# Two of the three matmuls of a split product made one of 512 columns, with the main sum and the corrections apart in a bank

## The chip, the cores and the metric

The kernel runs on one NeuronCore of a Trainium2 chip. The metric is the device time of one execution in microseconds (us). Engines: PE is TensorE, which multiplies, PEld its weight loads; DVE is VectorE, ACT ScalarE, POOL GpSimd, SP the engine that starts the DMAs. A bank is one of eight pieces of PSUM, TensorE's output memory: 2 KB on each of 128 partitions, 512 fp32 numbers.

## The reference, cut to what matters

256 tokens x of 1024 numbers go through two hybrid layers and then through one block of another kind, all in fp32:

```python
def hybrid_layer(x, norm_g, w_in, ...):
    p = split_columns(rmsnorm(x, norm_g) @ w_in)
    qk = silu(causal_dwconv(concat([p['ml_q'], p['ml_k']]), ...))
    hm = mlstm_chunkwise(...)
    hg = gla_chunked(heads(p['gla_q']), heads(p['gla_k']), ...)
    dk = rmsnorm(heads(p['dsa_k']), dsa_k_g)
    hd = dsa_sparse_attention(dq, dk, ..., topk)
    y = concat([y_ml, y_gla, y_dsa]) @ w_out
    return x + y

h = h + 0.5 * swiglu(rmsnorm_2(h), w_gate, w_up, w_down)
z = rmsnorm_2(h) @ w_in
# attention and a spatial gating of z, each through its w_branch, gated by sigmoid(n @ w_gate + b_gate), through w_out
h = h + 0.5 * swiglu(...)
```

Nearly all of the work is products of the 256 normed tokens with weight matrices that come from HBM once.

## The kernel before, in words

**Products.** A product keeps fp32's accuracy by splitting both factors into a rounded half and what is left of it (`hi` and `lo` of the weights, `xh` and `xl` of x), both in TensorE's faster fp32 type, and adding up three matmuls: wh with xh, wh with xl, wl with xh (`mm3`, L136).

**Units.** Weights come in units of 512 KB, in the order of their use, 362 in all (`weights`, L101): SP starts the DMA, ACT rounds the unit to `hi` (L112), DVE subtracts to get `lo` (L113). Five `hi`/`lo` pairs and three raw units fit, so casts run a few units ahead of PE.

**Two kinds of projection.** `proj_a` (L143) holds x in the array and moves 512 weight columns; its output is [token, 512 columns], in one bank for each of the two tokens' halves (t = 0 and 1; the prediction calls them the first and second token). `proj_b` (L173) holds 128 x 128 weights in the array and moves the 256 tokens; its output is [128 columns, n, 256 tokens], n = 2 column groups of one unit each in one bank. A unit of `proj_b` has eight k-steps of 128 rows each, 24 matmuls.

**PSUM.** Accumulators of the projections come from a pool `pj` of four banks (`acc`, L76), which go round: the next one waits until the oldest has been read for the last time. Another four banks, `mx`, serve everything else. `proj_b` returns its bank, and whoever uses the product reads it there: an ACT copy or scale (L358, L373, L374, L628, L875, L877), a tanh and a DVE product (L384 on, the FFN's `gated` at L836), a DVE operation in `mix` (L913).

**Stages.** `layer` (L344) works through the projections dq, iq, misc, dk, gq, gk, dv, dz and then those of the mLSTM heads (mq, mk, mv, mo, mz); smaller work (norms, gates, top-k selection, attention, recurrences) stands in generators (`start`, `tick`, L118 to L129) that go on by one step after each unit. Around the place of interest: `dsa_k` (L509) squares each token half of the keys dk (ACT), sums (DVE, `hss`, L498), takes the root (L184, DVE and POOL), and multiplies dk by it (DVE, `ks`, L517); later `ks` is transposed on PE (`kTp`). `ml_gates` (L581) makes `cd`, which PE turns into `cdp`, and DVE copies to `cdT` (L610). `dsa_select` (L442) does the top-k selection on DVE (L477 to L485). `ffn` (L829) has 9 passes with fg and fu, then its last projection; `mix` (L866) has v2p, qk2p, vgp, ugp, eight gatep, and the two branches (brp), each brp accumulator from one unit, with 4 k-steps for each of its two column groups.

**Order.** The kernel is written stage after stage; a scheduler then puts the instructions of each engine into one fixed order by priorities (weights run ahead by `high_priority`). On the chip each engine works through its order and waits for semaphores where a step depends on another engine.

## Time and profile before

| | |
|---|---|
| median of 3 runs | 1162.52 us (1160.75 to 1163.16) |
| the profiled execution | 1161.34 us, its span 1159.6 us |
| PE busy | 1134.9 us (98%), 7114 matmuls |
| DVE busy | 778.5 us (67%), 1138 instructions |
| ACT busy | 591.9 us (51%), 854 instructions |
| HBM read | 201.20 MB, 175 GB/s |

The span runs from the first instruction to the last. Busy shares of different engines overlap in time. A matmul's own duration in the rows (284 ns for 256 columns) is longer than the distance between two starts, since matmuls are pipelined; the cost of one is read from the distance. In a wait, the name behind the arrow is the instruction that came last before the wait ended.

### The profile page before, as it was taken

How to read it: one execution, taken by the hardware profiler on the slowest of the kernel's cores; microseconds unless marked ns; L12 is line 12 of the kernel's file. 1: busy time of each engine (PE TensorE's matmuls, PEld its weight loads, DVE VectorE, ACT ScalarE, POOL GpSimd, SP SyncE). 2: the span in 40 equal slices, each digit the busy share in tenths (PEclk: the TensorE clock that was granted, in tenths of full speed). 3: DMA queues.
4: the chain of work that ended last, by engine and by line, in shares of the span. 5: the costliest groups of instructions: out<-in, count | busy, mean ns of one | idle time of the engine just before them, and what ended most of it. 6: DMA issues, size and time to landing. Idle time of an engine off the chain costs nothing.

```text
span 1159.6 us, 18084 instructions
## 1 busy us (share of the span) xinstructions
PE 1134.9 (98%) x7114; PEld 1012.1 (87%) x7114; DVE 778.5 (67%) x1138; ACT 591.9 (51%) x854; POOL 94.6 (8%) x133
## 2 busy tenths in 40 slices
PE   8989999999999999999999999999999999999997
PEld 5878889997798978999788999888989997999986
DVE  5696897785668879778656655546585476656543
ACT  5645755564465575456444444435464445444432
POOL 1012111111011201111100000000010000000000
PEclk9999999999999999999999999999999999999999
DMA  7846445555575644455557566666753665665662
GB/s 268 270 143 195 144 139 162 167 175 171 162 206 151 197 142 125 148 166 168 173 157 226 180 182 185 189 191 192 210 165 110 182 187 179 197 182 183 184 196 75
DMA packets 59309, 203.57 MB, mean 176 GB/s; under 512 B 6668, under 2 KB 9620, under 8 KB 59224
## 3 DMA queue, kind: packets, MB, share of 16 engines
q1 hardware_dynamic: 59224, 202.42, 57.6%
q8 instruction: 56, 0.92, 0.3%
q14 instruction: 29, 0.24, 0.1%
HBM read 201.20 MB, written 2.11 MB: 175 GB/s over the span
## 4 chain that ended last, share of the span: by engine, by line
PE 91%; DVE 5%; ACT 1%; issue 1%; POOL 1%; DMA 1%; SPq 0%; DVEq 0%; POOLq 0%; ACTq 0%
PE op L141 19%; PE fg L141 11%; PE fu L141 11%; PE gatep L141 4%; PE mk L141 4%; PE mq L141 4%; PE mv L141 4%; PE mz L141 4%; PE mo L141 3%; PE dv L141 2%; PE brp L141 2%; PE qk2p L141 2%; PE dz L141 2%; PE iq L141 2%; PE gr L141 2%; PE gv L141 2%
## 5 line engine op out<-in xcount | busy, mean ns | idle before, releaser
L113 DVE TENSOR_TENSOR lo<-raw,hi 128x1024 fp32r<-128x1024 f32 x362 | 447.3, 1236 | 283.7 <-ACT hi L112 282.6
L112 ACT CAST hi<-raw 128x1024 fp32r<-128x1024 f32 x362 | 379.4, 1049 | 450.4 <-PE op L141 95.4
L141 PE MATMUL fu<-xh,hi 128*128 128x256 f32 x288 | 81.7, 284 | 0.0
L141 PE MATMUL fg<-xh,lo 128*128 128x256 f32 x288 | 81.5, 283 | 0.0
L141 PE MATMUL fg<-xl,hi 128*128 128x256 f32 x288 | 81.5, 283 | 0.0
L141 PE MATMUL fu<-xh,lo 128*128 128x256 f32 x288 | 81.5, 283 | 0.0
L141 PE MATMUL fg<-xh,hi 128*128 128x256 f32 x288 | 81.5, 283 | 0.0
L141 PE MATMUL fu<-xl,hi 128*128 128x256 f32 x288 | 81.5, 283 | 0.0
L141 PE MATMUL op<-hi,hh 128*128 128x512 f32 x176 | 68.6, 390 | 0.0
L141 PE MATMUL op<-hi,hl 128*128 128x512 f32 x176 | 68.6, 390 | 0.0
L141 PE MATMUL op<-lo,hh 128*128 128x512 f32 x176 | 68.5, 389 | 0.0
L141 PEld LDWEIGHTS fg<-xh,hi 128*128 128x128 f32 x288 | 55.3, 192 | 0.1
L141 PEld LDWEIGHTS fg<-xl,hi 128*128 128x128 f32 x288 | 55.3, 192 | 0.1
L141 PEld LDWEIGHTS fg<-xh,lo 128*128 128x128 f32 x288 | 55.3, 192 | 0.0
L141 PEld LDWEIGHTS fu<-xl,hi 128*128 128x128 f32 x288 | 55.3, 192 | 0.0
L141 PEld LDWEIGHTS fu<-xh,hi 128*128 128x128 f32 x288 | 55.3, 192 | 0.0
L141 PEld LDWEIGHTS fu<-xh,lo 128*128 128x128 f32 x288 | 55.3, 192 | 0.0
L284 POOL TENSOR_TENSOR r<-r,mhalf 128x1 f32<-128x1 f32 x12 | 6.7, 554 | 560.8 <-DVE r L283 560.8
L141 PE MATMUL op<-hi,yh 128*128 128x512 f32 x128 | 51.0, 398 | 0.0
L141 PE MATMUL op<-hi,yl 128*128 128x512 f32 x128 | 50.0, 391 | 0.0
L141 PE MATMUL op<-lo,yh 128*128 128x512 f32 x128 | 49.9, 390 | 0.0
L635 DVE SCALAR_TENSOR_TENSOR cacc<-pad,cols,cacc 128x256 f32<-128x256 f32 x96 | 41.8, 480 | 0.1
(403 smaller groups left out, 2983.1 us busy)
## 6 DMA issues: line engine op xcount, KB each, us to landing
raw<-in_w SPq DMA_DIRECT2D x362, 512.0 KB, 3.6
x<-in_x SPq DMA_DIRECT2D x2, 512.0 KB, 5.1
g_bc<-in_norm_g SPq DMA_DIRECT2D x2, 512.0 KB, 4.5
mlg<-in_ml_norm_g SPq DMA_DIRECT2D x2, 512.0 KB, 5.6
skew<-strips SPq DMA_DIRECT2D x4, 256.0 KB, 5.0
pen<-skew SPq DMA_DIRECT2D x8, 128.0 KB, 3.4
mb<-M SPq DMA_DIRECT2D x2, 512.0 KB, 4.4
g_bc<-in_ffn_norm SPq DMA_DIRECT2D x2, 512.0 KB, 5.6
```

What stands on the lines that cost most here:

```text
L112: nc.scalar.copy(hi, raw)
L113: nc.vector.tensor_sub(lo, raw, hi.bitcast(F32))
L141: self.nc.tensor.matmul(out, lhsT=lhsT, rhs=rhs, start=first and i == 0, stop=last and i == 2)
L284: nc.gpsimd.tensor_tensor(r, r, self.mhalf[:, 0:1], ALU.pow)
L635: nc.vector.scalar_tensor_tensor(acc[:, c, :], pad[:, c, 1 + i:1 + i + S], w(i), acc[:, c, :], ALU.mult, ALU.add)
```

## The change

`xh` and `xl` now lie side by side for each k-step (`x2`, [128, 8, 2, 256]). `mm2` takes the place of `mm3` in `proj_b` and in the branches of `mix`: wh meets xh and xl in one matmul of 512 columns, so that the product with xh (the main sum) gets the first 256 columns of a bank, and the product with xl the other 256; then wl meets xh, 256 columns, added to the second half (the corrections). An accumulator of two column groups so takes two banks. `pj` is two accumulators of two banks each, for `proj_a`, where the two banks are the two token halves, and for `out_proj`, too. `merged` adds up: ACT copies (or scales) the corrections to a tile `low`, DVE adds the main sum and `low` into SBUF. Users of a product read this SBUF tile. New tiles `s2` hold some of them; `ones` and `cd` share space with others. The rest of the diff, cut here, is that sharing.

```diff
         self.gap(pool("mid"), 64)
-        self.t2 = pool("t2", 7)
-        self.gap(pool("tail"), 384)
+        self.t2 = pool("t2", 8)
+        self.gap(pool("tail"), 256)
         self.stage = None
-        self.pj = pool("pj", 4, space=PSUM)
+        self.pj = pool("pj", 2, space=PSUM)
         self.mx = pool("mx", 4, space=PSUM)
...
-    def acc(self, shape, name):
-        return self.pj.tile(shape, F32, tag="pj", name=name)
+    def acc(self, name):
+        return self.pj.tile([P, 2, 512], F32, tag="pj", name=name)
...
+    def s2(self, shape, name):
+        return self.work(shape, name, 6, tag="s2")
...
-        ps = [self.acc([P, 512], f"{name}{t}") for t in range(2)]
+        two = self.acc(name)
+        ps = [two[:, t, :] for t in range(2)]
         if by_token is None:
...
-    def proj_b(self, x, name, n=2):
-        ps = self.acc([P, n, S], name)
+    def proj_b(self, x, name, out, scale=None, bias=None):
+        nc = self.nc
+        n = out.shape[1]
+        ps = self.acc(name)
         for c in range(n):
...
             for k in range(KT):
-                ww = [z[:, P * k:P * (k + 1)] for z in w]
-                self.mm3(ps[:, c, :], ww, [z[:, k, :] for z in x], False, k == 0, k == KT - 1)
+                self.mm2(ps[:, c, :], [z[:, P * k:P * (k + 1)] for z in w], self.x2[:, k], k == 0, k == KT - 1)
             self.tick()
-        return ps
+        self.merged(out, ps[:, :n], scale, bias)
+        return out
+    def mm2(self, out, w, x, first, last):
+        wh, wl = w
+        both = x.rearrange("p z t -> p (z t)")
+        self.nc.tensor.matmul(out, lhsT=wh, rhs=both, start=first, stop=False)
+        self.nc.tensor.matmul(out[:, S:], lhsT=wl, rhs=x[:, 0, :], start=False, stop=last)
+    def merged(self, out, ps, scale=None, bias=None):
+        nc = self.nc
+        n = out.shape[1]
+        low = self.tmp([P, n, S], "low")
+        if scale is None:
+            nc.scalar.copy(low, ps[:, :, S:])
+            if bias is None:
+                nc.vector.tensor_tensor(out, ps[:, :, :S], low, ALU.add)
+            else:
+                nc.vector.scalar_tensor_tensor(out, ps[:, :, :S], bias, low, ALU.add, ALU.add)
+        else:
+            nc.scalar.mul(low, ps[:, :, S:], scale)
+            nc.vector.scalar_tensor_tensor(out, ps[:, :, :S], scale, low, ALU.mult, ALU.add)
...
         g = self.row_bc(g_src, D, "g_bc")
-        xh = self.big.tile([P, KT, S], F32R, tag="xh", name="xh")
-        xl = self.big.tile([P, KT, S], F32R, tag="xl", name="xl")
+        self.x2 = self.big.tile([P, KT, 2, S], F32R, tag="x2", name="x2")
+        xh, xl = (self.x2[:, :, i, :] for i in range(2))
...
         done = self.begin_next()
-        ps = [[self.acc([P, 512], f"op{h}{t}") for t in range(2)] for h in range(2)]
+        two = [self.acc(f"op{h}") for h in range(2)]
+        ps = [[two[h][:, t, :] for t in range(2)] for h in range(2)]
         n = nk // 2
...
         for u in range(2):
-            ps = self.proj_b(x, "iq")
-            nc.scalar.copy(iqT[:, 2 * u:2 * u + 2, :], ps)
-        ps = self.proj_b(x, "misc", 1)
+            self.proj_b(x, "iq", iqT[:, 2 * u:2 * u + 2, :])
         ms = self.work([P, S], "ms")
-        nc.vector.tensor_scalar_add(ms, ps[:, 0, :], self.col("misc", 1, l))
-        ik2 = self.work([P, S], "ik2")
+        self.proj_b(x, "misc", ms.unsqueeze(1), bias=self.col("misc", 1, l))
+        self.ikcd = ik2 = self.work([P, S], "ikcd")
         nc.sync.dma_start(ik2[64:128, :], ms[0:64, :])
...
         gqk = self.t4([P, 2, 2, S], "gqk")
-        nc.scalar.mul(gqk[:, 0], self.proj_b(x, "gq"), 0.125)
-        nc.scalar.copy(gqk[:, 1], self.proj_b(x, "gk"))
+        self.proj_b(x, "gq", gqk[:, 0], 0.125)
+        self.proj_b(x, "gk", gqk[:, 1])
         dv = self.proj_a(x, "dv")
...
         for u in range(2):
-            ps = self.proj_b(x, "dz")
+            ps = self.proj_b(x, "dz", self.tmp([P, 2, S], "zdz"))
             th = self.tmp([P, 2, S], "th_dz")
...
             qk = self.t4([P, 2, 2, S], "qk")
-            self.conv(self.proj_b(x, "mq"), l, h, qk[:, 0])
-            self.conv(self.proj_b(x, "mk"), l, 4 + h, qk[:, 1])
+            self.conv(self.proj_b(x, "mq", self.padded()), l, h, qk[:, 0])
+            self.conv(self.proj_b(x, "mk", self.padded()), l, 4 + h, qk[:, 1])
             return self.start(self.ml_head(h, qk[:, 0], qk[:, 1], v1, hp))
...
-    def conv(self, ps, l, j, out):
-        nc = self.nc
-        pad = self.tmp([P, 2, S + 4], "pad")
-        nc.gpsimd.memset(pad[:, :, 0:4], 0.0)
-        nc.scalar.copy(pad[:, :, 4:], ps)
+    def padded(self):
+        self.pad = self.tmp([P, 2, S + 4], "pad")
+        self.nc.gpsimd.memset(self.pad[:, :, 0:4], 0.0)
+        return self.pad[:, :, 4:]
+    def conv(self, _, l, j, out):
+        nc = self.nc
+        pad = self.pad
         acc = self.tmp([P, 2, S], "cacc")
...
         for j in range(9):
-            g = self.proj_b(x, "fg")
-            u = self.proj_b(x, "fu")
+            g = self.proj_b(x, "fg", self.s2([P, 2, S], "fg"))
+            u = self.proj_b(x, "fu", self.s2([P, 2, S], "fu"))
             s = gated(f(g), f(u), 512)
...
         for u in range(4):
-            ps = self.proj_b(x, "qk2p")
-            if u < 2:
-                nc.scalar.mul(qk[:, 2 * u:2 * u + 2, :], ps, 0.125)
-            else:
-                nc.scalar.copy(qk[:, 2 * u:2 * u + 2, :], ps)
-        at = [self.work([P, 4, S], f"at{z}", dtype=F32R) for z in "hl"]
-        gm = [self.work([P, 4, S], f"gm{z}", dtype=F32R) for z in "hl"]
+            self.proj_b(x, "qk2p", qk[:, 2 * u:2 * u + 2, :], 0.125 if u < 2 else None)
+        at2, gm2 = (self.work([P, 4, 2, S], z, dtype=F32R) for z in ("at2", "gm2"))
+        at, gm = ([z[:, :, i, :] for i in range(2)] for z in (at2, gm2))
         self.start(self.attention(qk, vs, at))
...
         for u in range(8):
-            ps = self.proj_b(x, "gatep")
+            ps = self.proj_b(x, "gatep", self.s2([P, 2, S], "gatep"))
             for c in range(2):
...
         ml = self.work([P, 8, S], "ml", dtype=F32R)
-        for br, y in enumerate((at, gm)):
+        for br, y in enumerate((at2, gm2)):
             for j in range(0, 8, 2):
                 w = self.weights()
-                ps = self.acc([P, 2, S], "brp")
+                acc = self.acc("brp")
                 for c in range(2):
...
                         o = 256 * k + P * c
-                        self.mm3(ps[:, c, :], [z[:, o:o + P] for z in w], [z[:, k, :] for z in y], False, k == 0, k == 3)
+                        self.mm2(acc[:, c, :], [z[:, o:o + P] for z in w], y[:, k], k == 0, k == 3)
+                ps = self.s2([P, 2, S], "brs")
+                self.merged(ps, acc)
                 js = slice(j, j + 2)
```

What it moves, in the order of each engine's instructions. First PE in layer 0, from the last matmul of gq to the transposes of the keys, before (gk in two units, cdp between them; names carry buffer numbers):

```order
L141 MATMUL gq_616<-xh_104,lo_684 128x256
L141 MATMUL gk_722<-xh_104,hi_725 128x256
...
L141 MATMUL gk_722<-xh_104,lo_726 128x256
L609 MATMUL cdp_754<-ident_72,cd_552 128x64 [waits Activation_49,Pool_49]
L609 MATMUL cdp_757<-ident_72,cd_552 128x64 [waits Activation_49]
L141 MATMUL gk_722<-xh_104,hi_773 128x256
...
L141 MATMUL gk_722<-xh_104,lo_774 128x256
L196 MATMUL kTp_809<-ident_72,ks_470 128x128 [waits DVE_49,Activation_49]
L196 MATMUL kTp_809<-ident_72,ks_470 128x128 x3
L196 MATMUL kTp_815<-ident_72,ks_470 128x128 [waits DVE_49,Activation_49]
L196 MATMUL kTp_815<-ident_72,ks_470 128x128 x3
L141 MATMUL dv0_822<-hi_826,xh_104 128x512
```

And the same place with the change (L197 and L198 are the two matmuls of `mm2`, L227 the transposes):

```order
L197 MATMUL gq_576<-x2_104,hi_635 128x512
L198 MATMUL gq_576<-x2_104,lo_636 128x256
L640 MATMUL cdp_692<-ident_72,ikcd_429 128x64 [waits DVE_49,Activation_49,Pool_49]
L640 MATMUL cdp_695<-ident_72,ikcd_429 128x64 [waits Activation_49]
L227 MATMUL kTp_739<-ident_72,ks_432 128x128 [waits DVE_49,Activation_49]
L227 MATMUL kTp_739<-ident_72,ks_432 128x128 x3
L197 MATMUL gk_668<-x2_104,hi_671 128x512 [waits DVE_49]
L198 MATMUL gk_668<-x2_104,lo_672 128x256
...
L197 MATMUL gk_668<-x2_104,hi_711 128x512
L198 MATMUL gk_668<-x2_104,lo_712 128x256
L227 MATMUL kTp_745<-ident_72,ks_432 128x128 [waits Activation_49]
L227 MATMUL kTp_745<-ident_72,ks_432 128x128 x3
```

Both cdp and the first four transposes now stand ahead of gk, and the first gk matmul has a wait for DVE, which is for the `ks` of the second token half, the last reader of dk.

DVE at the same place, from the reduction of the first token half to the second `ks`, before:

```order
L498 TENSOR_REDUCE hss<-sq 128x4 [waits Activation_49,Pool_49]
L477 SCALAR_TENSOR_TENSOR sc<-relu,iw,sc 128x256 [waits DVE_49]
L517 TENSOR_TENSOR ks<-dk_472,rk 128x512 [waits Pool_49]
L477 SCALAR_TENSOR_TENSOR sc<-relu,iw,sc 128x256 [waits DVE_49]
L498 TENSOR_REDUCE hss<-sq 128x4 [waits Activation_49]
L113 TENSOR_TENSOR lo<-raw,hi 128x1024 [waits DMAHW7_49,PE_49,Activation_49]
L517 TENSOR_TENSOR ks<-dk_473,rk 128x512 [waits Pool_49]
L479 MEMSET sc 64x64 [waits DVE_49]
L610 COPY cdT<-cdp 128x64 [waits PE_49]
L484 MAX m_712<-sc 128x8 [waits DVE_49]
L610 COPY cdT<-cdp 128x64 [waits PE_49]
```

And with the change:

```order
L529 TENSOR_REDUCE hss<-sq 128x4 [waits Activation_49,Pool_49]
L508 SCALAR_TENSOR_TENSOR sc<-relu,iw,sc 128x256 [waits DVE_49]
L548 TENSOR_TENSOR ks<-dk,rk 128x512 [waits Pool_49]
L508 SCALAR_TENSOR_TENSOR sc<-relu,iw,sc 128x256 [waits DVE_49]
L641 COPY cdT<-cdp 128x64 [waits PE_49]
L510 MEMSET sc 64x64 [waits DVE_49]
L641 COPY cdT<-cdp 128x64 [waits PE_49]
L118 TENSOR_TENSOR lo<-raw,hi 128x1024 [waits DMAHW7_49,Activation_49]
L529 TENSOR_REDUCE hss<-sq 128x4 [waits Activation_49]
L515 MAX m_656<-sc 128x8 [waits DVE_49]
L548 TENSOR_TENSOR ks<-dk,rk 128x512 [waits Pool_49]
```

Now cdT, the memset and a `lo` stand between the first `ks` and the reduction of the second half.

PE in the mix stage, where the second accumulator of gatep begins, before:

```order
L141 MATMUL gatep_8332<-xl_7272,hi_8389 128x256
L141 MATMUL gatep_8332<-xh_7271,lo_8390 128x256
L141 MATMUL gatep_8442<-xh_7271,hi_8445 128x256
L141 MATMUL gatep_8442<-xl_7272,hi_8445 128x256
L141 MATMUL gatep_8442<-xh_7271,lo_8446 128x256
```

With the change:

```order
L969 MATMUL al1_7756<-qk2_7155 128x256 [waits PE_49]
L969 MATMUL al0_7755<-qk2_7155 128x256
L969 MATMUL al1_7756<-qk2_7155 128x256
L197 MATMUL gatep_7720<-x2_6624,hi_7723 128x512 [waits DVE_49]
L198 MATMUL gatep_7720<-x2_6624,lo_7724 128x256
```

It follows other matmuls now and has a wait for DVE. That wait is for the fifth row of this piece of DVE's order, the add of the first gatep accumulator:

```order
L1020 TENSOR_TENSOR vg_7350<-vg_7350,g5_7655 128x512 [waits DVE_49]
L998 TENSOR_SCALAR gesq_7612<-gesq_7612 128x512 [waits Activation_49]
L1021 TENSOR_TENSOR vg_7350<-vg_7350,b5_7657 128x512 [waits DVE_49]
L999 TENSOR_TENSOR gesq_7612<-gesq_7612,ugp_7492 128x512 [waits DVE_49]
L208 TENSOR_TENSOR gatep_7621<-gatep_7622,low_7714 128x512 [waits Activation_49]
L986 TENSOR_TENSOR ats_7586<-aO_7743,srec_7604 128x2x64 [waits PE_49]
L1001 SCALAR_TENSOR_TENSOR ug_7491<-gesq_7612,ugp_7492 128x512 [waits Activation_49]
L986 TENSOR_TENSOR ats_7586<-aO_7743,srec_7604 128x2x64
```

The add stands between the two last reads of ugp, the gelu of its second part (L999 and L1001, in the kernel before L966 and L968).

## Rows read from the trace of the kernel before

**Rows 1.** The page's parts 1 and 2, whole program.

```profile
span 1159.6 us, 18084 instructions
...
PE 1134.9 (98%) x7114; PEld 1012.1 (87%) x7114; DVE 778.5 (67%) x1138; ACT 591.9 (51%) x854; POOL 94.6 (8%) x133
...
PEclk9999999999999999999999999999999999999999
```

**Rows 2.** The page's part 4, the chain that ended last, by engine.

```profile
PE 91%; DVE 5%; ACT 1%; issue 1%; POOL 1%; DMA 1%; SPq 0%; DVEq 0%; POOLq 0%; ACTq 0%
```

**Rows 3.** That chain by time: start, us, engine, tile, line.

```profile
620.33 10.88 PE fu L141 x48
...
643.59 5.76 PE fg L141 x48
```

**Rows 4.** Waits of PE: tile and line, waited for, us in total, times, longest.

```profile
PE kTp L196 <- DVE cdT L610: 5.1, 2, 3.2
```

**Rows 5.** Timeline of PE, layer 0: start, us, line, tiles.

```profile
62.30 0.28 PE L141 MATMUL gq<-xh,lo 128*128 128x256 f32 x1
62.42 0.28 PE L141 MATMUL gk<-xh,hi 128*128 128x256 f32 x1
...
65.39 0.33 PE L609 MATMUL cdp<-ident,cd 64*128 64x64 f32 x2
...
68.62 0.60 PE L196 MATMUL kTp<-ident,ks 128*128 128x128 f32 x4
72.39 0.99 PE L196 MATMUL kTp<-ident,ks 128*128 128x128 f32 x4 [3.17 <-DVE cdT L610]
73.03 0.78 PE L141 MATMUL dv<-hi,xh 128*128 128x512 f32 x1
```

**Rows 6.** Timeline of DVE, layer 0, the two key tokens.

```profile
65.29 0.68 DVE L498 TENSOR_REDUCE hss<-sq 128x4 f32<-128x512 f32 x1
...
67.56 0.69 DVE L517 TENSOR_TENSOR ks<-dk,rk 128x512 f32<-128x512 f32 x1 [1.20 <-POOL rk L189]
...
68.56 0.68 DVE L498 TENSOR_REDUCE hss<-sq 128x4 f32<-128x512 f32 x1
...
71.55 0.69 DVE L517 TENSOR_TENSOR ks<-dk,rk 128x512 f32<-128x512 f32 x1 [1.17 <-POOL rk L189]
```

**Rows 7.** Timelines of DVE and PE, layer 1, the same place.

```profile
364.67 0.69 DVE L517 TENSOR_TENSOR ks<-dk,rk 128x512 f32<-128x512 f32 x1 [1.20 <-POOL rk L189]
...
368.66 0.69 DVE L517 TENSOR_TENSOR ks<-dk,rk 128x512 f32<-128x512 f32 x1 [1.18 <-POOL rk L189]
...
369.50 0.63 PE L196 MATMUL kTp<-ident,ks 128*128 128x128 f32 x4 [1.88 <-DVE cdT L610]
369.88 0.48 PE L141 MATMUL dv<-hi,xh 128*128 128x512 f32 x1
```

**Rows 8.** Stretches: window, us, busy by engine, clock, DMA.

```profile
72.50:75.90 3.40, 3.40 (x11) 2.82 (x11) 3.40 (x12) 1.16 (x2) 0.00 (x0) 0.50 0.39 120
...
372.00:375.00 3.00, 3.00 (x15) 2.47 (x14) 3.00 (x10) 1.06 (x1) 0.00 (x0) 1.00 0.61 175
```

**Rows 9.** Single lines: ns min/median/max, and the page's part 5.

```profile
L841 DVE TENSOR_TENSOR fs<-fs,fu x22: 680/687/689, 631.2 to 1093.0; 128x512 f32<-128x512 f32 x22
...
L373 ACT ACTIVATE gqk<-gq x2: 589/592/594, 63.4 to 361.8; 128x512 f32<-128x512 f32 x2
...
L113 DVE TENSOR_TENSOR lo<-raw,hi 128x1024 fp32r<-128x1024 f32 x362 | 447.3, 1236 | 283.7 <-ACT hi L112 282.6
```

**Rows 10.** Stretches of the mix stage, columns as above.

```profile
860.00:873.00 13.00, 13.00 (x106) 12.16 (x103) 12.36 (x20) 8.52 (x19) 3.86 (x8) 1.00 0.56 171
918.60:941.70 23.10, 23.10 (x195) 23.10 (x194) 17.03 (x20) 10.85 (x13) 0.00 (x0) 1.00 0.60 182
```

**Rows 11.** Timeline of DVE in the mix stage.

```profile
869.55 0.67 DVE L968 SCALAR_TENSOR_TENSOR ug<-gesq,ugp 128x512 f32<-128x512 f32 x1
...
924.66 0.69 DVE L913 SCALAR_TENSOR_TENSOR merged<-gates,brp 128x512 f32<-128x512 f32 x1 [0.69 <-PE brp L141]
```

More of the change, by code (lines that the diff above doesn't have):

```diff
@@ L229, in loads @@
         self.keep = self.held("keep")
-        self.ones = self.const.tile([4, S], F32, tag="ones", name="ones")
+        self.ones = self.gwa[0:4, 0, :]
         nc.gpsimd.memset(self.ones, 1.0)
@@ L592, in ml_gates @@
         nc.vector.tensor_tensor_scan(B, self.ones[0:4, :], lf, 0.0, ALU.mult, ALU.add)
-        cd = self.work([64, S], "cd")
+        cd = self.ikcd[0:64]
         nc.gpsimd.memset(cd, 0.0)
```

## The prediction

> **What bounds it now.** I read the busy table first: TensorE (PE) works 1134.9 us of a span of 1159.6 at a granted clock that reads 9 in every slice, so little is left between its instructions [rows 1]. The chain of waits says the same: 91% is PE, 5% VectorE (DVE) [rows 2]. Its pieces give the price of a matmul: 48 of the 256-column kind in 5.76 us, one start every 120.0 ns, and 48 of 512 columns in 10.88 us, one every 226.7 ns [rows 3]. So 256 columns more cost 106.7 ns, and 13.3 ns of each matmul do not depend on its columns. At 2.4 GHz, the upper of the clock's two levels, 256 columns take just those 106.7 ns. Where PE waits for another engine by name, the largest entry is the transposes of the keys (kTp), 5.1 us in two waits [rows 4]. That place, and what surrounds it on DVE, is where the change is decided.
>
> **The change, part by part.** *Fewer matmuls.* One k-step of mm3 with the weights stationary is three matmuls of 256 columns, 3 x 120.0 = 360.0 ns; mm2 makes it one of 512 and one of 256, 226.7 + 120.0 = 346.7 ns [rows 3]. That saves 13.3 ns per k-step. A unit has 8 k-steps. Per layer 29 units are multiplied so (iq 4, misc 1, gq 2, gk 2, dz 4, mq 8, mk 8), in each FFN 36, in the mix stage 8 (qk2p), 16 (gatep) and 8 (brp, 4 k-steps for each of two column groups): 58 + 72 + 32 = 162 units, 1296 k-steps, 17.3 us, 0.107 us per unit. With PE the bound this is the time gained wherever no new wait swallows it.
>
> *The adding up.* Each accumulator now costs one ScalarE (ACT) copy and one DVE add. I price them by ACT reading 512 elements from a bank, 592 ns, and DVE combining such a bank with an SBUF tile, 687 ns [rows 9]. 84 pairs of column groups make 84 x 0.687 = 58 us on DVE, which is idle a third of the span, and some 33 us on ACT, where 28 of the copies replace old ones. In an FFN a pair of accumulators takes PE 4 x 2.77 = 11.1 us; DVE then does four lo of 1.236 and five adds and products of about 0.69, 8.4 us [rows 9]. That fits, and each add has the 5.5 us of the next accumulator to finish in. I cost the adds there at nothing; the cover is those 5.5 us. In mq, mk, dz and qk2p the same holds.
>
> *Two accumulators for four banks: the keys.* The bound is no longer work but release. dk fills one of the two accumulators, gq the other, so gk must wait until dk has been read for the last time, by the ks of the second token. Before, gk had a free bank and followed gq in the next slot (62.42 after 62.30), and filled the time in which the keys were normed; the wait for kTp was what was left [rows 5]. Now PE stands still from the end of gq but for cdp and four kTp. When does ks end? Before, it started at 67.56 and 71.55, 2.27 and 2.99 us after its reduction [rows 6]. The chain starts a little later (I take 0.25 us, for merged copies of misc and gq on ACT and DVE ahead of it), and now, as the order shows, the two cdT copies, a memset and the 1.2 us lo stand between the first ks and the second reduction. So: first ks ends 67.56 + 0.69 + 0.25 = 68.5; some 0.9 for sc, cdT and memset, 1.2 for lo gives 70.6; reduction to ks 2.3 to 3.0, and 0.69, gives 73.6 to 74.3. I take 73.6, since the 2.99 us of before held the lo that now stands ahead of the reduction. gk then takes 16 x 0.3467 = 5.55 and four transposes about 0.45, and dv starts at 79.6 instead of 73.03 [rows 5]: **+6.6 us**, in which the savings of the 9 units up to there are used up. The same sum in layer 1, from 364.67 and 368.66 [rows 7], has gk start at about 370.7 and dv at 376.7, not 369.88: +6.8.
>
> *The clock.* In layer 0 PE waited 3.17 us before 72.39 [rows 5], and from 72.50 its granted clock was 0.50 for 3.40 us; in layer 1 it waited 1.88 us [rows 7], and the clock stayed at 1.00 [rows 8]. 0.50 is the lower level, 1.2 GHz. With a standstill longer than layer 0's, layer 1 should fall to it too: 3.4 us at half speed lose 1.7; the bounds are nothing, and twice that if the clock falls after each half of the standstill. Layer 0 pays 1.7 already. Layer 1: **+8.5**. The 20 units after it in each layer give 20 x 0.107 = **-2.1** each.
>
> *The same in the mix stage.* The second gatep accumulator now waits for the add of the first, which stands on DVE just ahead of the second ug; that ran at 869.55 before [rows 11], and DVE is busy 12.36 of 13.00 us there [rows 10], so a lo that now comes earlier (1.2) and the add (0.69) push it to 871.4, and the adds before it to some 872. Before, half of that accumulator, one unit of 8 x 0.36 = 2.9 us, was done by then. Attention's matmuls fill part of the gap; between nothing and 2.9 I take the middle, **+1.6** by that point with the savings of three units used up, then 13 units x 0.107 = **-1.4**. v2p's second half waits for the ACT copy of the first, **+0.2**. qk2p gives 8 x 0.107 = **-0.85**. In brp an accumulator lasts 2.77 us, and DVE must do lo (1.236), add and merge (2 x 0.69) in it, 2.6; the second branch adds two more operations. DVE had 17.03 busy of 23.10 us [rows 10] and gets 8 x 0.69 = 5.5 more, 22.5. The add comes behind cast and lo, so some is late: 0.85 gained, about 1.65 lost, **+0.8**. The bounds are -0.85 (all in time) and +4 (each of eight 0.5 late, as the 0.69 us that DVE waited before a merge [rows 11] is nearly used up).
>
> *FFNs:* 36 x 0.107 = **-3.85** each.
>
> The sum: 6.6 + 8.5 - 4.2 + 1.6 - 1.4 + 0.2 - 0.85 + 0.8 - 7.7 = **+3.5 us**. The profiled execution took 1161.34; it becomes 1164.9. That execution lies 1.2 us under the median of the runs shown, 1162.52, so I predict **1166 us**. A difference under 0.2%, 2.3 us, can't be told from none here.
>
> Of the fixed part of a matmul the Trainium skill ("TensorE: Matmul & The Clock Gate", Part 1, "Wait — 56ns, not 53.3ns?") says it is about 2.5 ns at the upper clock. This trace differs: 13.3 ns with these operands. By the page's figure the 1296 k-steps would save an estimated 3.2 us, not 17.3. Another rule speaks against the change: independent groups should rotate through different PSUM banks, so that their evacuation overlaps the next group's matmuls (the Trainium skill, "Perfetto Trace Analysis", Matmuls). The trace agrees in that gk ran behind gq while dk was still unread.
>
> **The rivals.**
> (1) *The waits are short.* DVE and ACT drain dk sooner, as PE's standstill frees nothing that they need; or its clock holds. For it: DVE waited 1.2 us ahead of ks, for the root on GpSimd [rows 6], so it has time there. Against: its order is fixed, and even before the second ks ended at 72.2, 9.8 us behind gq [rows 5, 6]. If half of the 15.1 us were lost: 1158.5. If none: 1166 - 15.1 - 2 for the units up to dv = 1149. Chance 0.2 together, 0.06 for the second.
> (2) *More waits.* Beyond the keys and gates, DVE is late in brp at its bound, +3, the clock falls once more at gatep, +1.7, and ks ends 1.5 later in both layers as the gates' chain holds cdT up, +3: 1174. For it: DVE's 12.36 of 13.00. Chance 0.2.
> (3) *The fixed part stays.* If the 13.3 ns are paid for the weights' exchange beside a short stream, so that a 512-column matmul between two short ones saves nothing, then the 15 us of units still counted above are not gained: 1166 + 15 = 1181. Against: the 512-column groups exchange their weights for every matmul too, and 226.7 less 120.0 is what the columns alone take [rows 3]. By the 2.5 ns of the Trainium skill ("TensorE: Matmul & The Clock Gate", Part 1) it would be an estimated 1178. Chance 0.05.
> (4) *The change does not do as it says*, as the 512 columns run in two passes: the same time as (3), and its chance is in there.
>
> **The numbers.** My own case has 0.55: 1162 to 1170, as ks may end 1.5 us sooner or later in each layer and brp has its bounds. Of it 0.38 is slower by over 0.2% (above 1164.9), 0.17 the same. Rival (1) gives 0.17 to faster and 0.03 to the same, (2) and (3) 0.25 to slower: faster 0.17, same 0.20, slower 0.63. Leaving out the lower 0.08 and the upper 0.08, the range is 1153 to 1175.
>
> **What would show it.** Right: matmul starts 226.7 and 120 ns apart in every weights-stationary unit, a wait of PE for ks of some 4 to 8 us in each layer ahead of gk, a slice of lower clock behind it also in layer 1, FFNs shorter by 3.8 us each, and DVE some 55 us busier. Wrong: gk that starts before 70 in layer 0, k-steps not at 347 ns, or waits for adds inside the FFN loop.

## The result, and the profile after

The change made the kernel slower: 1180.37 us (median of 4 runs, 1179.42 to 1181.22) against 1161.63 before (1160.75 to 1163.16), a ratio of 1.016 with a 95% interval of 1.0142 to 1.0177. The forecast was 1166, with a range of 1153 to 1175. The direction was right, the size was not: 18.7 us were lost where some 4 were expected.

The page of the profile after (span, the engines' busy times from part 1, the clock by slices), to set beside [rows 1]:

```profile
span 1177.8 us, 15638 instructions
...
PE 1136.6 (97%) x5818; PEld 945.5 (80%) x5818; DVE 830.7 (71%) x1222; ACT 622.4 (53%) x912; POOL 88.7 (8%) x133
...
PEclk8989999999998999999999999999998999999999
```

PE works as long as before, with 5818 matmuls in place of 7114, and the span is 18.2 us longer; the clock's digit is 8 in four slices: the start, the keys of both layers, and gatep. PE's waits after (as [rows 4]: tile and line, waited for, us, times, longest):

```profile
PE kTp L227 <- DVE ks L548: 9.0, 2, 4.5
PE gk L197 <- DVE ks L548: 6.6, 2, 3.3
...
PE st L684 <- DVE qk L673: 1.8, 4, 0.5
PE apT L227 <- ACT lg L597: 1.6, 1, 1.6
...
PE brp L197 <- DVE brs L208: 0.8, 1, 0.8
```

The kTp entry is 9.0 us in place of 5.1, gk has one of 6.6, and st (a product of the mLSTM heads), apT (a transpose of mix's attention) and brp are new. These rows hold 14.7 us more than the one row that they had before [rows 4]. They don't show what half clock costs behind them. So the table takes the start time of each projection in the two profiles (1177.8 and 1159.6 us of span), and gives for each stage the difference at its end less that at its start:

| stage | forecast, us | measured, us |
|---|---|---|
| start to iq | 0 | +2.3 |
| iq to dv, layer 0 | +6.6 | +6.1 |
| dv to layer 1 | -2.1 | -0.5 |
| layer 1 to dv | +8.5 | +7.5 |
| dv to FFN 1 | -2.1 | +1.0 |
| FFN 1 | -3.85 | -1.9 |
| FFN 1's last projection, v2p to ugp | -0.65 | +0.1 |
| gatep | +0.2 | +5.0 |
| brp | +0.8 | +1.9 |
| FFN 2 and before it | -3.85 | -3.5 |
| end | 0 | +0.2 |
| sum | +3.5 | +18.2 |

**The keys, as forecast.** PE at the place of [rows 5], layer 0 with the change:

```profile
64.67 0.34 PE L640 MATMUL cdp<-ident,ikcd 64*128 64x64 f32 x2
69.53 1.09 PE L227 MATMUL kTp<-ident,ks 128*128 128x128 f32 x4 [4.53 <-DVE ks L548]
73.94 0.79 PE L197 MATMUL gk<-x,hi 128*128 128x512 f32 x1 [3.32 <-DVE ks L548]
...
81.47 0.71 PE L146 MATMUL dv<-hi,x 128*128 128x512 f32 x2
```

gk starts at 73.94 (forecast 73.6, which had no late start), dv at 81.47. DVE there, beside [rows 6]:

```profile
68.69 0.69 DVE L548 TENSOR_TENSOR ks<-dk,rk 128x512 f32<-128x512 f32 x1 [1.20 <-POOL rk L220]
...
69.98 1.21 DVE L118 TENSOR_TENSOR lo<-raw,hi 128x1024 fp32r<-128x1024 f32 x1
71.11 0.68 DVE L529 TENSOR_REDUCE hss<-sq 128x4 f32<-128x512 f32 x1
...
73.19 0.69 DVE L548 TENSOR_TENSOR ks<-dk,rk 128x512 f32<-128x512 f32 x1 [1.07 <-POOL rk L220]
```

The first ks is 1.13 us later than in [rows 6], less than the 2.3 by which iq was late; then cdT and lo stand ahead of the second reduction, and 2.08 us after that comes the second ks. The clock, as in [rows 8] (columns as there):

```profile
73.90:77.00 3.10, 3.06 (x9) 2.67 (x10) 3.10 (x14) 0.00 (x0) 0.00 (x0) 0.50 0.49 198
...
377.80:381.00 3.20, 3.16 (x10) 2.68 (x11) 3.20 (x14) 0.00 (x0) 0.00 (x0) 0.50 0.47 189
...
887.00:893.00 6.00, 6.00 (x21) 4.71 (x21) 4.57 (x9) 1.51 (x3) 0.40 (x2) 0.50 0.00 0
12.00:18.00 6.00, 5.16 (x15) 3.75 (x15) 6.00 (x11) 3.06 (x4) 0.77 (x1) 0.53 0.89 268
```

Behind each standstill at the keys the clock was 0.50 for some 3 us, now in layer 1 too, as the forecast had it. It also fell at gatep and in the first matmuls, where the forecast did not have it.

Part of the agreement in layer 0 is luck. gk starts 45.4 us after iq where the forecast had 47.4, since the late start only moved the first ks by 1.1 us; the wait took up the rest. And the half clock, which the forecast left in dv, now lies in gk: from gk to dv it is 7.5 us in place of the forecast's 6.0, and dv itself is 1.3 shorter than before, in the row "dv to layer 1".

**Gatep, not as forecast.** PE in the mix stage, from the end of the first gatep accumulator to the start of the second:

```profile
880.44 0.28 PE L198 MATMUL gatep<-x,lo 128*128 128x256 f32 x1
882.28 1.91 PE L227 MATMUL apT<-ident,lg 128*128 128x128 f32 x8 [1.56 <-ACT lg L597]
884.76 0.43 PE L984 MATMUL aO<-dvs,pT 128*128 128x64 f32 x2 [0.57 <-ACT pT L978]
...
890.53 0.79 PE L197 MATMUL gatep<-x,hi 128*128 128x512 f32 x1
```

In the kernel before, the second accumulator's matmuls stood between the apT and filled the softmax's latency:

```profile
866.49 0.40 PE L196 MATMUL apT<-ident,lg 128*128 128x128 f32 x2
866.64 0.36 PE L141 MATMUL gatep<-xh,hi 128*128 128x256 f32 x1
...
867.91 0.42 PE L196 MATMUL apT<-ident,lg 128*128 128x128 f32 x2
```

Now the second takes the first's banks, which are free only after the add, and the add needs the first's corrections (low), which ACT has to copy:

```profile
881.63 0.50 ACT L597 ACTIVATE lg<-lg,smax 128x256 f32<-128x256 f32 x1
...
884.12 1.07 ACT L978 COPY pT<-apT 128x512 f32<-128x512 f32 x2
885.08 0.60 ACT L206 COPY low<-gatep 128x512 f32<-128x512 f32 x1
```

```profile
887.03 0.68 DVE L208 TENSOR_TENSOR gatep<-gatep,low 128x512 f32<-128x512 f32 x1
```

low stands on ACT behind four exps with their sums, and pT; it comes at 885.08, 4.6 us after the start of the accumulator's last matmul, and the add follows at 887.03. So in PE's order apT, aO and al now stand ahead of the second accumulator. PE waits for the exps (1.56 us) and for pT (0.57), from 887 on its clock is at half, and the second accumulator starts at 890.53, right behind the last al. By then the add had been done for 2.8 us: what costs is the order in which PE gets its work, and the clock.

**The FFNs, half as forecast in one of them.** The first matmuls of two accumulators that follow each other, in FFN 1 and in FFN 2 of the same run:

```profile
659.60 0.40 PE L197 MATMUL fg<-x,hi 128*128 128x512 f32 x1
...
665.26 0.40 PE L197 MATMUL fu<-x,hi 128*128 128x512 f32 x1
...
1044.12 0.39 PE L197 MATMUL fg<-x,hi 128*128 128x512 f32 x1
...
1049.66 0.39 PE L197 MATMUL fu<-x,hi 128*128 128x512 f32 x1
```

5.66 us and 5.54 us for 16 k-steps; over the whole loops it is 5.653 and 5.547, so 353 and 347 ns for one k-step, against 360 before. All of FFN 1 ran at the first, all of FFN 2 but its first two accumulators at the second. The forecast's 346.7 is the second as a sum, though not in its parts: the 512 columns took 232 ns and the 256 took 115, where it had 226.7 and 120.0.

### The profile page after: what moved, and what is told of

The parts are those of the page before. It is cut to its first block, busy times and chain, and to the rows that moved or that the text cites. A ratio compares the mean times of both kernels' runs of the same rounds, so it can differ in the third digit from the quotient of the medians.

```text
span 1177.8 us, 15638 instructions
## 1 busy us (share of the span) xinstructions
PE 1136.6 (97%) x5818; PEld 945.5 (80%) x5818; DVE 830.7 (71%) x1222; ACT 622.4 (53%) x912; POOL 88.7 (8%) x133
## 4 chain that ended last, share of the span: by engine, by line
PE 88%; DVE 7%; ACT 2%; issue 1%; DMA 1%; POOL 1%; SPq 0%; DVEq 0%; POOLq 0%; ACTq 0%
PE op L146 19%; PE fg L197 6%; PE fu L197 6%; PE mz L146 4%; PE mv L146 3%; PE fg L198 3%; PE fu L198 3%; PE gatep L197 3%; PE mk L197 3%; PE mo L146 2%; PE mq L197 2%; PE dq L146 2%; PE gv L146 2%; PE fg L146 2%; PE dv L146 2%; PE fu L146 2%
## 5 line engine op out<-in xcount | busy, mean ns | idle before, releaser
L197 PE MATMUL fu<-x,hi 128*128 128x512 f32 x288 | 101.9, 397 | 0.0
L197 PE MATMUL fg<-x,hi 128*128 128x512 f32 x288 | 101.7, 396 | 0.0
L198 PE MATMUL fg<-x,lo 128*128 128x256 f32 x288 | 80.4, 279 | 0.0
L198 PE MATMUL fu<-x,lo 128*128 128x256 f32 x288 | 80.4, 279 | 0.0
L197 PEld LDWEIGHTS fg<-x,hi 128*128 128x128 f32 x288 | 54.1, 188 | 13.1
L197 PEld LDWEIGHTS fu<-x,hi 128*128 128x128 f32 x288 | 54.1, 188 | 13.0
L198 PEld LDWEIGHTS fg<-x,lo 128*128 128x128 f32 x288 | 54.2, 188 | 0.1
L198 PEld LDWEIGHTS fu<-x,lo 128*128 128x128 f32 x288 | 54.2, 188 | 0.0
L197 PE MATMUL mq<-x,hi 128*128 128x512 f32 x128 | 46.7, 404 | 0.0
L197 PE MATMUL gatep<-x,hi 128*128 128x512 f32 x128 | 46.6, 407 | 0.0
L197 PE MATMUL mk<-x,hi 128*128 128x512 f32 x128 | 46.1, 400 | 0.4 <-DVE sz_z L720 0.4
```

What stands on the lines that cost most here:

```text
L197: self.nc.tensor.matmul(out, lhsT=wh, rhs=both, start=first, stop=False)
L198: self.nc.tensor.matmul(out[:, S:], lhsT=wl, rhs=x[:, 0, :], start=False, stop=last)
```

## The experiments

The theories were: A, the loss is the release of two accumulators where there were four banks; B, it is the adding up on ACT and DVE. Apart from these, it had to be shown that the matmuls do save time.

**1. Two accumulators alone.** From the kernel before:

```diff
-        self.pj = pool("pj", 4, space=PSUM)
+        self.pj = pool("pj", 2, space=PSUM)
...
+    def half(self, n, name):
+        return self.acc(name)[:, 0, :n * S].rearrange("p (a b) -> p a b", a=n)
...
-        ps = self.acc([P, n, S], name)
+        ps = self.half(n, name)
```

> Two accumulators of two banks each, as in the change, but three matmuls of 256 columns into one bank and nothing added up: the release of banks alone. Theory A (the loss is release: gk waits for the last reader of dk, gatep for ugp's bank): gk starts some 11 us behind gq in both layers, as with the change (73.9 and 377.8 there); 15 us in all at the keys, since no saving is set against it, some 3 at gatep: about 1180. Theory B (the loss is the adding up on DVE and ACT): 1162 to 1168.

Measured: 1176.44 us, ratio 1.0128 (1.0113 to 1.0143), 15.1 us over the 1161.34 of before. PE at the keys:

```profile
62.83 0.33 PE L614 MATMUL cdp<-ident,cd 64*128 64x64 f32 x2
69.32 1.09 PE L200 MATMUL kTp<-ident,ks 128*128 128x128 f32 x4 [6.15 <-DVE ks L522]
70.40 0.58 PE L144 MATMUL gk<-xh,hi 128*128 128x256 f32 x1
```

The standstill is there without any adding up: from cdp at 62.83 to kTp at 69.32, and then the time of gk behind it. By the borders of the stages dv is 5.3 and 4.9 us later within layer 0 and 1 (15 in all were expected there), gatep 6.4 us longer (3 expected), and dv itself in layer 0, which ran at half clock before [rows 8], 1.3 shorter; all else is within 0.7. So release alone costs more than was expected of it at gatep and less at the keys. At gatep the first accumulator goes to ACT's tanh there, behind the same exps and pT.

At the keys the release is not the same as with the change. Here gk takes the accumulator of gq, which is free after one read by ACT, behind the second sq:

```profile
69.76 0.59 ACT L378 ACTIVATE gqk<-gq 128x512 f32<-128x512 f32 x1
```

That ends at 70.35, gk starts at 70.40, and it waits for the first ks but not for the second. With the change gq is free only after an add on DVE, which comes behind the second ks:

```profile
74.20 0.68 DVE L213 SCALAR_TENSOR_TENSOR gqk<-gq,low 128x512 f32<-128x512 f32 x1
```

So there gk takes dk's accumulator and waits for the second ks as well: the row of 6.6 us among PE's waits, which run 1 does not have.

**2. The adding up alone.** From the change, with four single banks and mm3:

```diff
-        self.pj = pool("pj", 2, space=PSUM)
+        self.pj = pool("pj", 4, space=PSUM)
...
+        self.mm3(out, w, [x[:, i, :] for i in range(2)], False, first, last)
...
+        h = 0.5 * (1.0 if scale is None else scale)
+        nc.scalar.mul(low, ps, h)
+        nc.vector.scalar_tensor_tensor(out, ps, h, low, ALU.mult, ALU.add)
```

> Four single banks and three matmuls as before, but each product halved and added to itself (ACT scales half of it into a tile, DVE adds the other half, one more DVE operation for misc): the adding up alone. Theory A: 1162 to 1166, gk right behind gq, only the first-needed products late. Theory B: the stages where DVE is dense (the mLSTM heads, gatep) are longer by what the change lost there, some 3 us per layer from mq to the next stage and 4 at gatep: 1170 to 1175.

Measured: 1168.87 us, ratio 1.0064 (1.0049 to 1.0079), 7.5 us over before and between the two theories. At gatep and brp it lost nothing (0.0 at both borders). From mq to the next stage it lost 2.0 us in each layer, less than theory B had. Of the rest, 2.4 lie ahead of iq, where the clock fell as with the change, and 2.1 between the start of layer 1 and its mq (layer 0 there: -0.8), 1.6 of them in dv, where the clock fell (0.50 from 374.9 to 378.2). At the keys gk stands ahead of both kTp again, and the second kTp waits 2.33 us in layer 0. What PE waits for in the mLSTM heads, and did not before:

```profile
PE st L675 <- DVE qk L664: 1.7, 2, 0.8
```

qk is the end of the convolution on DVE, which begins with the added-up mq or mk. Adding up costs some 4 us of its own, in the mLSTM heads. DVE is busy there far above its mean in [rows 1]; the stretch in the kernel before (columns as in [rows 8], the third busy time is DVE's):

```profile
141.00:193.00 52.00, 51.41 (x338) 46.26 (x337) 45.34 (x73) 26.20 (x39) 9.68 (x14) 1.00 0.50 150
```

**3. The saving taken back.** From the change:

```diff
-        both = x.rearrange("p z t -> p (z t)")
-        self.nc.tensor.matmul(out, lhsT=wh, rhs=both, start=first, stop=False)
+        if first:
+            self.nc.tensor.matmul(out, lhsT=wh, rhs=x.rearrange("p z t -> p (z t)"), start=True, stop=False)
+        else:
+            self.nc.tensor.matmul(out[:, :S], lhsT=wh, rhs=x[:, 0, :], start=False, stop=False)
+            self.nc.tensor.matmul(out[:, S:], lhsT=wh, rhs=x[:, 1, :], start=False, stop=False)
```

> The change as it is, but from the second k-step of each unit on (the first of brp's four and of the others' eight stays) wh meets xh and xl in two matmuls of 256 columns: the saving taken back. If a k-step of mm2 saves 7 to 14 ns (353 to 346 ns against 360) where PE is the bound: 10 to 14 us more than the change, about 1192, and the FFN accumulators 5.75 us apart again instead of 5.65 and 5.55. Rival, the fixed part of a matmul is not saved: 1180.

Measured: 1189.9 us, ratio 1.0244 to before (1.0227 to 1.0262), 9.5 us over the change. Two accumulators of FFN 1:

```profile
662.36 0.40 PE L197 MATMUL fg<-x,hi 128*128 128x512 f32 x1
...
668.11 0.40 PE L197 MATMUL fu<-x,hi 128*128 128x512 f32 x1
```

5.75 us. So the saving is real: 9.5 us, a little under the 10 to 14 expected. The first k-step of each group keeps the long matmul, so 1126 of the 1296 k-steps are taken back, which at 13.3 ns would be 15.0 us. The rival of the forecast by which nothing is saved falls.

The three do not add up: 15.1 + 7.5 - 9.5 = 13.1, not 18.7. What is missing appears only where both parts meet. Most of it lies at the keys: within the two layers dv is 8.2 and 8.3 us later in run 3, against 5.3 and 4.9 in run 1 and -1.1 and 0.5 in run 2. The wait of gk for the second ks, 3.3 us in each layer, comes only with both: four banks are enough to do without it (run 2), and without the add gq's accumulator is free sooner (run 1). brp shows it, too: 0.0 in run 1, 0.0 in run 2, 1.9 with the change, since only there the adding up sits between an accumulator and the next that needs its bank.

**4. Keys copied out.** From the change:

```diff
-        p4 = ps.rearrange("p (h d) -> p h d", h=4)
+        nc.scalar.copy(ks[:, t, :], ps)
+        k4 = ks[:, t, :].rearrange("p (h d) -> p h d", h=4)
-        self.head_rms(p4, rk, 1.0 / 128)
-        k4 = ks[:, t, :].rearrange("p (h d) -> p h d", h=4)
-        nc.vector.tensor_tensor(k4, p4, rk.unsqueeze(2).to_broadcast([P, 4, P]), ALU.mult)
+        self.head_rms(k4, rk, 1.0 / 128)
+        nc.vector.tensor_tensor(k4, k4, rk.unsqueeze(2).to_broadcast([P, 4, P]), ALU.mult)
```

> The change, with dk copied by ACT from its banks to the tile ks at once, squared and scaled from there, so that its accumulator is free long before gk. Theory A: gk starts right behind gq again (near 64.7 and 352 + the offset of layer 1), the 3 us before the second kTp stay, 6 us less in layer 0 and 7 in layer 1: about 1167. Theory B: the DVE order is as late as before, so kTp takes over most of the wait: 1174 to 1180.

Measured: 1166.69 us, ratio 1.0047 (1.0031 to 1.0064), 13.7 us less than the change. PE, layer 0:

```profile
64.24 0.28 PE L198 MATMUL gq<-x,lo 128*128 128x256 f32 x1
64.36 0.39 PE L197 MATMUL gk<-x,hi 128*128 128x512 f32 x1
...
73.49 1.08 PE L227 MATMUL kTp<-ident,ks 128*128 128x128 f32 x4 [2.48 <-DVE sc L510]
74.23 1.20 PE L146 MATMUL dv<-hi,x 128*128 128x512 f32 x2
```

gk is back behind gq, 0.12 us after it, and the kTp wait is 2.48. Within layer 0 dv comes 0.9 us earlier than before, in layer 1 0.4 later. That puts 6.1 - (-0.9) = 7.0 and 7.5 - 0.4 = 7.1 us of the change's loss down to one late accumulator. The total of 13.7 is these 14.1 only roughly: both FFNs gave 3.7 in this run, 1.7 more than with the change, and 2.3 were lost again behind the keys (1.1 in layer 0's dv, at half clock again, and 1.2 ahead of layer 1's gv, which run 7 comes back to).

**5. The FFNs alone.** From the kernel before, with one bank for each column group:

```diff
+    def proj_c(self, x, name, out, scale=None):
+        for c in range(n):
+            ps = self.acc([P, 512], f"{name}{c}")
...
+            low = self.tmp([P, S], "low")
...
+                nc.vector.tensor_tensor(out[:, c, :], ps[:, :S], low, ALU.add)
...
-            g = self.proj_b(x, "fg")
-            u = self.proj_b(x, "fu")
+            g = self.proj_c(x, "fg", self.s2([P, 2, S], "fg"))
+            u = self.proj_c(x, "fu", self.s2([P, 2, S], "fu"))
```

> The kernel before with mm2 in the nine passes of the two FFNs alone: one bank for each column group (256 columns main sum, 256 corrections), four banks in the pool, each group added up by ACT and DVE; all else as before. If the saving is what the FFN of the change showed: 1.9 us less per FFN at 353 ns per k-step, 3.7 at 346; in all 4 to 7.4 us less than before, 1154 to 1157. Rival (adding up on 256 columns is too slow for DVE, or banks come back late): no gain, 1161.

Measured: 1156.35 us (1152.03 to 1159.23), ratio 0.9947 (0.9928 to 0.9966): 5.7 us less than before. Two accumulators that follow each other, in its FFN 1 and FFN 2:

```profile
659.71 0.39 PE L196 MATMUL fu<-x,hi 128*128 128x512 f32 x1
...
665.25 0.39 PE L196 MATMUL fg<-x,hi 128*128 128x512 f32 x1
...
1019.25 0.40 PE L196 MATMUL fg<-x,hi 128*128 128x512 f32 x1
...
1024.90 0.40 PE L196 MATMUL fu<-x,hi 128*128 128x512 f32 x1
```

Here FFN 1 has the short pitch (5.54) and FFN 2 the long (5.65), the other way round than with the change, and the stages gave 3.7 and 1.9. Which of the two pitches a loop gets is not a matter of the FFN.

**6. ugp copied out too.** From run 4's kernel:

```diff
+            uc = self.s2([P, 2, S], "ugc").rearrange("p a b -> p (a b)")
+            nc.scalar.copy(uc, ps[t])
-            self.gelu(ps[t], ug[:, t, :])
+            self.gelu(uc, ug[:, t, :])
```

> The change with dk copied out as in the run before, and ugp also copied out of its accumulator by ACT (two copies into SBUF, the gelu reads those), so that the second gatep accumulator need not wait for the first one's adding up. If the 5 us at gatep are that release: gatep to brp 57 us or less instead of 63.4, 6 us less: 1160 to 1161. Rival (ACT, with eight exps of the softmax ahead, is what makes it late whatever bank is free): the 5 us stay, 1166.

Measured: 1159.84 us, ratio 0.9982 (0.9972 to 0.9991), 6.9 us less than run 4's. gatep's stage went from 5.0 us longer than before to 0.7 shorter. PE there:

```profile
868.68 0.44 PE L227 MATMUL apT<-ident,lg 128*128 128x128 f32 x2
...
870.17 0.42 PE L227 MATMUL apT<-ident,lg 128*128 128x128 f32 x2
```

The apT matmuls have no wait any more and are again spread between those of the second gatep accumulator. The second accumulator takes ugp's banks now, which ACT's copies free early, and the first gatep product is added up as with the change. The release is the cause; ACT's queue is only what makes it so late.

**7. Three matmuls again where adding up costs more.**

```diff
+    def proj_d(self, x, name):
+        ps = self.half(2, name)
...
+                self.mm3(ps[:, c, :], ww, [self.x2[:, k, i, :] for i in range(2)], False, k == 0, k == KT - 1)
...
-            self.conv(self.proj_b(x, "mq", self.padded()), l, h, qk[:, 0])
+            self.conv(self.proj_d(x, "mq"), l, h, qk[:, 0])
```

(mk and brp in the same way; run 6's copies are in this kernel, too.)

> As the last, and mq, mk and brp again with three matmuls of 256 columns into one bank (of an accumulator of two), read from there: the places where the adding up cost more than the matmuls saved. Expected: 1 us less per layer from mq to the next stage and 2 less in brp: 1154 to 1157. Rival (the release of two accumulators costs there by itself): no better than 1160.

Measured: 1157.6 us, ratio 0.9962 (0.9949 to 0.9975). brp went from +2.0 to +0.3, and from mq to the next stage it was -0.1 and -0.2 in place of +0.9 and +1.1; the wait of st is gone. The total lies a little above the 1154 to 1157 expected. One late add is left:

```profile
PE gv L146 <- DVE zdz L221: 2.3, 2, 1.2
```

PE stands still ahead of gv in both layers, until the dz product in the accumulator that gv needs has been added up.

**8 and 9. Six warming matmuls,** in run 7's kernel (run 8) and in the one before (run 9):

```diff
-        for _ in range(4):
+        for _ in range(6):
```

> As the last, with six warming matmuls at the start instead of four. In the profiles so far the granted clock rose during the warming at 5.0 to 8.2 us, by chance, and where it rose before 6.7 PE then stood idle until 8.34, was at half clock from about 12 to 18 and reached iq 2 us later. If that idle time is the cause: iq starts near 26.3 in every run, 1 to 2 us less than the run with four, and less scatter. Rival: the clock falls all the same, no difference.

> The kernel before with six warming matmuls instead of four, nothing else: what of the last version's gain is the warming. If a start that falls to half clock is a matter of chance in the kernel before too: 0 to 1.5 us less than before, 1160.5 to 1162, with less scatter, and the last version keeps 4 to 6 us over it. Rival: all of the gain of that version is the start: 1156.

Measured: 1155.56 us (1155.12 to 1155.78), ratio 0.9941 (0.9929 to 0.9953), the lowest median (runs 5 and 10 reach as low); and 1161.98 in the kernel before, ratio 0.9995 (0.9983 to 1.0006), no difference. Two stretches of run 8's, the start and behind the keys of layer 1, and after them the second of run 7's:

```profile
12.00:18.00 6.00, 5.43 (x20) 3.91 (x19) 6.00 (x10) 3.06 (x4) 0.56 (x1) 0.72 0.92 262
...
370.50:373.50 3.00, 3.00 (x9) 2.35 (x9) 3.00 (x12) 1.03 (x2) 0.00 (x0) 0.57 0.74 246
```

```profile
370.50:373.50 3.00, 3.00 (x15) 2.47 (x14) 3.00 (x12) 1.48 (x3) 0.00 (x0) 1.00 0.85 259
```

At the start the clock still fell, only for less long (0.72 over the 6 us; 0.53 with the change). So idle time ahead of the first projection is not shown to be the cause, and the kernel before gained nothing. The two profiles show where run 8 is ahead of run 7: 1.3 us in all, 1.8 of them in FFN 2, where run 8 has the short pitch and run 7 the long; up to there run 8 is 0.4 behind. So nothing in them speaks for the warming. (The expectation has the clock rise at 5.0 to 8.2 us; in the profiles of the runs up to 7 the warming matmuls come closer together from 4.9 to 7.7 us on.)

**10. The other order in every second k-step** (512, 256, 256, 512 columns), in run 8's kernel:

```diff
+        elif first or not self.flip:
+            self.nc.tensor.matmul(out, lhsT=wh, rhs=both, start=first, stop=False)
+            self.nc.tensor.matmul(out[:, S:], lhsT=wl, rhs=x[:, 0, :], start=False, stop=False)
+        else:
+            self.nc.tensor.matmul(out[:, S:], lhsT=wl, rhs=x[:, 0, :], start=False, stop=False)
+            self.nc.tensor.matmul(out, lhsT=wh, rhs=both, start=False, stop=False)
```

> The best version with the two matmuls of mm2 in the other order in every second k-step (512, 256, 256, 512 columns). So far whole FFN loops ran at 353 or at 346 ns per k-step, the one or the other by chance. If the sequence of column counts makes that: one fixed pitch in both FFNs, 346 or less gives 1153 to 1155.5 in every run, 353 or more 1159. Rival (it is a matter of what PE did before the loop): both pitches are still seen, 1155.5.

Measured: 1156.44 us (1154.9 to 1158.93), ratio 0.995 (0.9932 to 0.9968). Accumulators in FFN 1:

```profile
656.59 0.39 PE L215 MATMUL fg<-x,hi 128*128 128x512 f32 x1
...
662.17 0.39 PE L215 MATMUL fu<-x,hi 128*128 128x512 f32 x1
```

5.58 us here and 5.57 in FFN 2, 348 ns per k-step in both. With this order one pitch was seen in the one profile, between the two; the time is not better than run 8's.

## Why the prediction was wrong

The step that failed is the cost of the adding up and of the release outside the keys. The forecast costed the adds at nothing in the mLSTM heads and took a middle value at gatep; these two came out 5.7 and 4.8 us above it, of the 14.7 by which the profile missed.

- **The bound, the keys: the mechanism right, the size partly by luck.** gk waits for the last reader of dk, and in layer 1 the clock falls behind it: 6.1 and 7.5 us against 6.6 and 8.5. Run 4 shows it by taking it away; in run 1, where gk is held up by gq's release instead, the two layers lost 5.3 and 4.9. In layer 0 two errors offset each other, as said above: the wait was shorter, as iq came late, and the half clock moved into gk. The rule of the Trainium skill that groups should rotate through different banks ("Perfetto Trace Analysis", Matmuls) agrees: with two accumulators in place of four, run 1 lost 15 us without any added work.
- **"In mq, mk, dz and qk2p the same holds": wrong for mq and mk, the largest miss, 5.7 us.** I costed the adds at nothing because an accumulator lasts 5.5 us. But there the add stands at the head of a chain on DVE (convolution, qk) that PE's st waits for. Run 2 shows 2.0 us per layer from the adds alone in the mLSTM heads, and run 7 takes the loss away. I had taken DVE's load from the whole span, where it is 67% [rows 1]; there it is 87% (45.3 of 52 us). From mq to the next stage the change lost 1.0 and 1.3 us, where 16 units in each layer were to save 1.7. The table's "dv to layer 1" hides part of it, as dv gained 1.3. dz's add is late, too, where PE comes early enough to see it (run 7).
- **Gatep: 4.8 us.** "I take the middle, +1.6" looked at DVE alone ("stands on DVE just ahead of the second ug") and said that attention's matmuls fill the gap. But the add waited for ACT's low first (885.08, behind four exps and pT), and attention's matmuls waited for ACT themselves (1.56 and 0.57 us), since what had covered that wait was the accumulator that now stands behind them. Then the clock fell. Run 1, which adds nothing up, lost 6.4 us there, and run 6 takes the loss away by freeing other banks early. The rows of before could have told that gatep stood between apT.
- **The saving: the mechanism right, the size chancy.** "13.3 ns per k-step" held in some loops; in others it was 6.7. That took 1.9 us in FFN 1. The Trainium skill's 2.5 ns of a matmul ("TensorE: Matmul & The Clock Gate", Part 1) does not fit here either way: even 347 ns is 27 more than 768 columns at 2.4 GHz.
- **brp: right in kind.** +1.9 against +0.8, inside the bounds (-0.85 to +4).
- **The start: 2.3 us not foreseen.** The clock fell in the first projection. It did so in the profiles of runs 2, 3, 4 and 6, too, for less long in 8, 9 and 10, and not in those of before, 1, 5 and 7; the kernel of run 7 has the change's first matmuls and still did not, that of run 9 has those of before and did. So it is no effect of the change that could be shown, but it lies in the profiled difference.
- **The range:** rival (2), "more waits", named brp and the clock at gatep and gave 1174. It left the mLSTM heads, the wait for ACT and the start out. That rival (3), in which nothing is saved, says 1181, next to the measured 1180, is chance: run 3 shows the saving.

## What to carry to other kernels

When a change makes an accumulator larger, list for each accumulator who reads it last and what is queued ahead of that reader on every engine that the release passes through, ACT's copy as well as DVE's add; a product whose reader is a long chain (a norm, a gelu) is best copied out at once, which here cost two ACT copies a time and gave back, by the borders of the stages, 14.1 us at the keys of two layers and 5.7 at gatep. An add on a second engine makes a release later, and with it decides which accumulator the next product takes: gk took gq's in run 1 and dk's with the change. Load on an engine is to be read from the stage, not the span. And a matmul that waits where it used to fill somebody else's latency costs twice: its own time and the wait that it covered.

## What the runs showed of the hardware

**Two pitches for the same loop.** A k-step of 512 and 256 columns took 353 ns or 347 ns. In the FFNs it changed only behind the first two accumulators, where other matmuls of PE come between, and then stayed to the end of the loop: with the change FFN 1 had the long one and FFN 2 the short one, in runs 5 and 7 it was the other way round, in runs 4, 6 and 8 both were short. In the long one a 512-column matmul takes 236 ns where it takes 232 in the short. Why stays open.

**The clock's rise and fall differ from execution to execution.** The warming matmuls run at half clock until it rises, and the row of their group shows when, by its length: 5.71 us with the change and 6.74 before, for the same eight. At the start and behind waits of 2 to 4 us at the keys the clock sometimes fell and sometimes did not: in layer 1 of runs 7 and 8, behind the same wait of 2.48 us, it was 1.00 and 0.57 (the rows above).

What a fall costs depends on what comes next. At the start it was 2.1 to 2.4 us up to iq in the profiles of the change and of runs 2, 3, 4 and 6, and 0.0 to 0.7 in those of runs 8, 9 and 10, where the clock came back sooner. Behind the keys it was 1.3 to 1.6 us in dv; but in run 8 the wait ahead of gv that run 7 has was gone for it, so that from dv to gv the two differ by only 0.2 and 0.4 us.
